# Two score blocks in one tick: head pairs of a projection group in a hybrid attention layer

## The chip, the cores and the metric

One core of a Trainium2 chip runs the whole program. The metric is the device time of one execution in microseconds (us), as the median of three runs. Beside the timed runs there is one execution under the hardware profiler; its rows give the start and length of every instruction of each engine.

## The reference

A decoder layer on 256 tokens of width 2048, in float32. Two groups of 16 heads of 64 stand side by side: group A attends in a sliding window of 128 with two shared key and value heads, ALiBi slopes and a learned sink per head; group B attends causally over all 256 tokens with a forget gate per head. Then come an output projection and a channel mixer.

```python
q_a, k_a, v_a, q_b, k_b, v_b, f_b = jnp.split(rmsnorm(x, g) @ w_in, cuts, axis=-1)
# group A, per head:  s = q k^T / 8 - slope * distance, inside the window
p = exp(s - m) / (sum(exp(s - m)) + exp(sink - m));  o_a = p v
# group B, per head:  s = q k^T / 8 + c[t] - c[s],  c = cumsum(log_sigmoid(f_b + b))
p = softmax(s);  o_b = p v
mix = concat(rmsnorm(o_a), rmsnorm(o_b)) @ w_out
x = x + rmsnorm(mix)
x = x + rmsnorm((gelu(conv(gate)) * conv(val)) @ w_down)
```

## The kernel before, in words

All large products are float32 products made of parts. A weight unit of 128 x 1024 floats is loaded from memory by the SP queue into one of five `raw` buffers; ScalarE (ACT) casts it to a high part `whi` (L112) and VectorE (DVE) subtracts to get a low part `wlo` (L115), each with five buffers. TensorE (PE) multiplies high by the high and low halves of the activations in one product of 512 columns (L253) and low by high in one of 256 columns (L258).

`proj_T` computes 256 output columns: in each of its two halves stand 16 products of L253 and 16 of L258, and four calls of `tick()`: after 6 and 12 of the L253, after 10 of the L258, and at the half's end, so eight ticks in all. The value projections (L309, `mm3`) and the output projection have ticks of their own. A tick runs whatever was registered for it by `later(n, f)`. In this way attention work is put in the middle of a projection, and since the PE queue is in program order, the tick fixes where it stands there. DVE, ACT, GpSimd (POOL) and SP get their order from a scheduler that moves with the program; each then executes in that order and waits in place.

A projection group makes the queries of 256 columns, which are two head pairs; there are four groups in each attention group. `attend` registers four steps for a pair at the ticks that `stages` gives:

- `tables`, three ticks ahead of the scores: POOL writes the bias of the pair into `p` (two buffers). In group B this begins with a small load `cb` (L578) on the SP queue, also two buffers.
- `scores` (L475): twelve small products on 64 rows, six for each head `e`, into two of the four PSUM banks tagged `att`. Then DVE adds the bias and takes the row maximum (L481, four of them), ACT takes the exponentials (L493, four), DVE adds the sink in group A (L489, L496), inverts the sums (L497) and scales `p` (L500, four).
- `transposes` (L510): six on PE into two `att` banks; ACT casts the high part `ph` (L312), DVE makes the low part `pl` (L313).
- `pv` (L522 and L524 in group A, L534 and L536 in group B): the value products into one `att` bank; ACT and DVE move the result to `oT` (L527, L530, L545, L546, L547), and POOL sums the squares (L551, L553).

Before the change `stages(n)` puts scores, transposes and value products at ticks n, n + 6 and n + 9. In group A the pairs have n = 6, 14, 22 and so on, eight ticks apart; in group B the first pair of a group has n = 3 and the second 11, counted from the end of the group's key projection, the second falling in the next projection. Queries and keys are moved out of PSUM by L440 (ACT), L441 (DVE) and L442 (POOL), and split by L312 and L313; a key pair takes one of three slots of the tile `keys`.

Of the kernel before, what the change touches and what calls it, by code (L numbers as in the profile page):

```python
# [31 lines left out]
def hybrid_layer(ctx: ExitStack, tc: tile.TileContext, x, pre_mix_g, w_in, b_forget, sinks,  # L32
# [16 lines left out]
    def bank(tag="acc"):  # L49
        return ps.tile([P, 512], F32, tag=tag, bufs=4, name="bank_" + tag)  # L50
# [9 lines left out]
    def later(n, f):  # L60
        todo.setdefault(now[0] + n, []).append(f)
# [116 lines left out]
    def rstd_of(ssq, n, out_tag):  # L178

        v = small.tile([P, 1], F32, tag="rv", name="rv")  # L180
        dve.tensor_scalar(v, ssq, 1.0 / n, EPS, op0=ALU.mult, op1=ALU.add)
        r = small.tile([P, 1], F32, tag=out_tag, bufs=2, name=out_tag)
        pool.tensor_tensor(r, v, mhalf, op=ALU.pow)
        return r
# [58 lines left out]
    def proj_T(w, c0, banks):  # L243

        for v in (0, 2):
            parts = [w_split(w_load(w_rows(w, u * 4, 4, c0, 256), 4, 256), still=True)
                     for u in (v, v + 1)]
            steps = [(u, a) for u in range(2) for a in range(4)]

            def high(u, a):  # L250
                kt = (v + u) * 4 + a
                for m, b in enumerate(banks):
                    pe.matmul(b, parts[u][0][:, a, m * P:(m + 1) * P], hT[:, kt, :],  # L253
                              start=(kt == 0), stop=(kt == KT - 1))

            def low(u, a):
                for m, b in enumerate(banks):
                    pe.matmul(b[:, 256:512], parts[u][1][:, a, m * P:(m + 1) * P],  # L258
                              hT[:, (v + u) * 4 + a, 0:256], start=False, stop=False)

            for n, (u, a) in enumerate(steps[:-1]):
                high(u, a)
                if n in (2, 5):
                    tick()
            for n, (u, a) in enumerate(steps):
                low(u, a)
                if n == 4:
                    tick()
            high(*steps[-1])
            tick()  # L270
# [40 lines left out]
    def split(hi, lo, src):  # L311
        act.copy(hi, src)  # L312
        dve.tensor_tensor(lo, src, hi.bitcast(F32), op=ALU.subtract)  # L313

    with tc.tile_pool(name="mixp", bufs=1) as mp:
# [37 lines left out]
        def scratch():  # L353
            rot[0] += 1
            i = 6 + rot[0] % 10
            return scr[:, i * 256:(i + 1) * 256]
# [80 lines left out]
        def evac_sum(b, dst, row):  # L437

            c = scratch()
            act.copy(c, b[:, 256:512])  # L440
            dve.tensor_tensor(dst, b[:, 0:256], c, op=ALU.add)  # L441
            pool.tensor_tensor(dst, dst, row, op=ALU.mult)  # L442

        def q_pair(b):
            q = scratch()
            evac_sum(b, q, rowq)
            qh = ap.tile([P, 256], F32R, tag="qh", bufs=6, name="qh")
            ql = ap.tile([P, 256], F32R, tag="ql", bufs=6, name="ql")
            split(qh, ql, q)
            return qh, ql  # L450

        def k_pair(b, i):
            k = scratch()
            evac_sum(b, k, rowk)
            split(khi[i], klo[i], k)
# [106 lines left out]
        def swa_pair(p, q, at):  # L562
            def table(t):
                for e in range(2):
                    slope = 2.0 ** (-8.0 * (2 * p + e + 1) / H)
                    pool.tensor_scalar(t[:, e, 0:256], dist, -slope, None, op0=ALU.mult)
                    pool.tensor_scalar(t[:, e, 256:384], dist[:, P:256], -slope, None,
                                       op0=ALU.mult)

            attend(p, q, p // 4, lambda t: vpa[:, t, p // 4, :], table, 2 * p, True, at,  # L570
                   True)
# [3 lines left out]
        def fox_pair(p, q, ki, at):  # L575
            def table(t):
                cb = ap.tile([P, 2, 256], F32, tag="cb", bufs=2, name="cb")
                sp.dma_start(cb.rearrange("p e k -> p (e k)"),  # L578
                             c_dram[2 * p:2 * p + 2, :].rearrange("e k -> (e k)")
                             .partition_broadcast(P))  # L580
                for e in range(2):
                    h = 2 * p + e
                    pool.tensor_scalar(t[:, e, 0:256], cb[:, e, :], -1.0, cq[:, 1, h:h + 1],
                                       op0=ALU.mult, op1=ALU.add)
                    pool.tensor_scalar(t[:, e, 256:384], cb[:, e, 0:P], -1.0, cq[:, 0, h:h + 1],
                                       op0=ALU.mult, op1=ALU.add)

                v = t[:, :, P:384]
                pool.affine_select(out=v, in_=v, compare_op=ALU.is_ge, fill=NEG, base=0,
                                   pattern=[[0, 4], [-1, P]], channel_multiplier=1)  # L590

            attend(8 + p, q, ki, lambda hl, t: vpb[:, hl, t, p, :], table, 2 * p, False, at)

        def stages(n):
            return n, n + 6, n + 9


        def kv_a():
# [21 lines left out]
        for g in range(4):  # L620
            if g == 0:
                b2 = bq0
            else:
                b2 = [bank(), bank()]
                proj_T(w_in, g * 256, b2)
            for m in range(2):
                swa_pair(2 * g + m, q_pair(b2[m]), stages(6 + 8 * (2 * g + m) - 8 * g))


        z = ap.tile([P, 2, H], F32, tag="z", name="z")  # L630
        for p0, npair, cols in ((0, 3, 384), (3, 3, 384), (6, 2, 272)):
            b2 = [bank(), bank()]
# [45 lines left out]
        def group_rstd(i, into):  # L678
            gbk = bank("att")
            for t in range(2):  # L680
                pe.matmul(gbk[:, t:t + 1], sqs[:, i, t * P:(t + 1) * P], ones[:, 0:1],
                          start=True, stop=True)
            for t in range(2):
                into.append(rstd_of(gbk[:, t:t + 1], 1024, f"rg{i}{t}"))

        rstd_a, rstd_b = [], []
        later(30, lambda: group_rstd(0, rstd_a))
        for g in range(4):
            bq = [bank(), bank()]
            proj_T(w_in, 1280 + g * 256, bq)  # L690
            qs = [q_pair(b) for b in bq]
            bk = [bank(), bank()]
            proj_T(w_in, 2304 + g * 256, bk)
            for m in range(2):
                ki = (2 * g + m + 2) % NK
                k_pair(bk[m], ki)
                fox_pair(2 * g + m, qs[m], ki, stages(3 + 8 * m))


        later(stages(11)[2] + 4, lambda: group_rstd(1, rstd_b))  # L700
        mix_sb = main.tile([P, 2, D], F32, tag="y", name="mix_sb")
        mix = [[mix_sb[:, t, n * 512:(n + 1) * 512] for n in range(4)] for t in range(2)]

# [528 lines left out]
```

## Time and profile before

| what | value |
|---|---|
| median of 3 runs | 1070.96 us (1070.4 to 1071.1) |
| the profiled execution | 1070.95 us |
| its span, first to last instruction | 1069.2 us |
| PE busy over the span | 1052.4 us, 98% |
| DVE busy | 843.4 us, 79% |
| ACT busy | 637.2 us, 60% |
| POOL busy | 224.8 us, 21% |
| mean granted TensorE clock | 0.997 |

The profiled execution agrees with the median to 0.01 us; 1.75 us of it lie outside the span. Attention work stands between 42 and 275 us: group A from 42 to 149 us, group B from 161 to 274 us. In a row of the timeline the first number is the start, the second the length of the merged row, then engine, line and tiles, and a count; a square bracket gives the idle time before it and what ended it. PE records overlap, because a product starts before the one ahead of it has ended, so the pace of PE is read from starts to starts and not from lengths.

### The profile page before, as it was taken

To read this page: it belongs to the slowest core of one execution; us is meant where nothing else is said; L and a number is where in the kernel's file an instruction comes from. 1 tells how busy PE (TensorE), PEld (TensorE's weight loads), DVE (VectorE), ACT (ScalarE), POOL (GpSimd) and SP (SyncE) were. 2 spreads that over 40 slices of the span, in tenths; PEclk is the share of its full clock that TensorE was granted. 3 is DMA by queue.
4 is the path that set the end of the run, shared out by engine and by line. 5 is a ranking of instruction groups with operands and counts; after the bars stand their busy time and mean duration, and the time that the engine had idled before them with its cause. 6 is when DMAs were issued, how large, how long until landed. Compare 5 with 4: busy or idle time off the path is not lost.

```text
span 1069.2 us, 16290 instructions
## 1 busy us (share of the span) xinstructions
PE 1052.4 (98%) x5890; PEld 912.9 (85%) x5890; DVE 843.4 (79%) x1369; ACT 637.2 (60%) x1096; POOL 224.8 (21%) x256
## 2 busy tenths in 40 slices
PE   9999999999999999999999999999999999999996
PEld 7889988887889988888888888888888888888785
DVE  5988877887567887787767989668777787788995
ACT  7766766666556765565655556446555565656561
POOL 3233343342022121221212000002121211200202
PEclk9999999999999999999999999999999999999998
DMA  8645657555873776665666566666566666685552
GB/s 291 206 120 174 180 160 210 161 153 156 300 248 106 266 229 188 192 190 181 211 186 191 192 203 209 215 187 197 167 209 190 190 191 195 192 301 191 167 175 79
DMA packets 154284, 207.08 MB, mean 194 GB/s; under 512 B 6844, under 2 KB 131036, under 8 KB 153180
## 3 DMA queue, kind: packets, MB, share of 16 engines
q1 hardware_dynamic: 153200, 203.37, 60.5%
q10 hardware_dynamic: 1004, 2.68, 0.6%
q8 instruction: 46, 0.75, 0.3%
q14 instruction: 34, 0.28, 0.1%
HBM read 201.68 MB, written 4.21 MB: 193 GB/s over the span
## 4 chain that ended last, share of the span: by engine, by line
PE 90%; DVE 4%; DMA 2%; issue 2%; POOL 1%; ACT 1%; SPq 0%; DVEq 0%; POOLq 0%; ACTq 0%
PE bank_acc L284 16%; PE bank_att L967 14%; PE bank_att L284 14%; PE bank_acc L309 12%; PE bank_acc L290 8%; PE bank_att L290 7%; PE bank_acc L253 6%; PE bank_acc L967 4%; PE bank_acc L258 3%; PE bank_att L475 1%; DVE wlo L313 1%; PE bank_att L510 1%; DVE wlo L115 1%; PE bank_acc L932 1%; DMA x_in<-in_x_dram 1%
## 5 line engine op out<-in xcount | busy, mean ns | idle before, releaser
L115 DVE TENSOR_TENSOR wlo<-raw,whi 128x1024 fp32r<-128x1024 f32 (+3 forms) x271 | 330.1, 1228 | 117.1 <-ACT whi L112 112.4
L112 ACT CAST whi<-raw 128x1024 fp32r<-128x1024 f32 (+3 forms) x270 | 273.3, 1029 | 124.4 <-issue 88.9
L899 POOL TENSOR_TENSOR room<-room,rowf 128x256 f32<-128x256 f32 x88 | 100.3, 1160 | 393.9 <-DVE room L898 392.1
L284 PE MATMUL bank_acc<-hT,whi 128*128 128x512 f32 x736 | 173.3, 390 | 0.0
L284 PEld LDWEIGHTS bank_acc<-hT,whi 128*128 128x128 f32 x736 | 136.5, 188 | 27.3
L967 PE MATMUL bank_att<-whi,G 128*128 128x512 f32 x488 | 156.2, 389 | 0.0
L284 PE MATMUL bank_att<-hT,whi 128*128 128x512 f32 x640 | 150.6, 390 | 0.0
L284 PEld LDWEIGHTS bank_att<-hT,whi 128*128 128x128 f32 x640 | 118.7, 188 | 23.8
L967 PEld LDWEIGHTS bank_att<-whi,G 128*128 128x128 f32 x488 | 91.6, 188 | 18.9
L967 PE MATMUL bank_att<-wlo,G 128*128 128x512 f32 x244 | 95.2, 390 | 2.4 <-DVE wlo L313 2.4
L290 PEld LDWEIGHTS bank_acc<-hT,wlo 128*128 128x128 f32 x736 | 89.3, 188 | 2.0
L290 PE MATMUL bank_acc<-hT,wlo 128*128 128x256 f32 x736 | 89.9, 279 | 0.0
L253 PE MATMUL bank_acc<-hT,whi 128*128 128x512 f32 x352 | 89.2, 396 | 0.0
L901 ACT ACTIVATE room<-room,cw 128x256 f32<-128x256 f32 x88 | 53.0, 602 | 60.6 <-POOL room L899 60.6
L309 PE MATMUL bank_acc<-whi,oT 128*128 128x512 f32 (+1 forms) x272 | 82.5, 380 | 0.0
L290 PEld LDWEIGHTS bank_att<-hT,wlo 128*128 128x128 f32 x640 | 77.6, 188 | 1.7
L290 PE MATMUL bank_att<-hT,wlo 128*128 128x256 f32 x640 | 77.9, 279 | 0.0
L903 DVE SCALAR_TENSOR_TENSOR room<-room,cw 128x256 f32<-128x256 f32 x88 | 62.4, 709 | 17.5 <-ACT room L901 17.3
L313 DVE TENSOR_TENSOR wlo<-raw,whi 128x1024 fp32r<-128x1024 f32 (+1 forms) x56 | 62.4, 1138 | 13.4 <-ACT whi L312 13.4
L253 PEld LDWEIGHTS bank_acc<-hT,whi 128*128 128x128 f32 x352 | 63.0, 188 | 11.3
L312 ACT CAST whi<-tb 128x1024 fp32r<-128x1024 f32 x42 | 44.0, 1050 | 45.0 <-PE bank_att L967 19.2
L312 ACT CAST whi<-raw 128x1024 fp32r<-128x1024 f32 (+1 forms) x56 | 52.4, 958 | 28.8 <-PE bank_att L967 22.2
(254 smaller groups left out, 1589.9 us busy)
## 6 DMA issues: line engine op xcount, KB each, us to landing
raw<-in_w_up_dram SPq DMA_DIRECT2D x176, 512.0 KB, 4.1
raw<-in_w_down_dram SPq DMA_DIRECT2D x58, 512.0 KB, 4.8
raw<-in_w_in_dram SPq DMA_DIRECT2D x51, 512.0 KB, 3.9
raw<-in_w_out_dram SPq DMA_DIRECT2D x32, 512.0 KB, 4.7
extra<-in_w_down_dram SPq DMA_DIRECT2D x20, 512.0 KB, 3.8
raw<-in_w_in_dram SPq DMA_DIRECT2D x16, 384.0 KB, 3.4
tb<-in_w_down_dram SPq DMA_DIRECT2D x10, 512.0 KB, 4.8
cb<-c_dram SPq DMA_DIRECT2D x8, 256.0 KB, 3.6
```

Of the source, the lines that this page charges most:

```text
L112: i1 = act.copy(hi[:, cs], raw[:, cs])
L115: i2 = dve.tensor_tensor(lo[:, cs], raw[:, cs], hi[:, cs].bitcast(F32), op=ALU.subtract)
L253: pe.matmul(b, parts[u][0][:, a, m * P:(m + 1) * P], hT[:, kt, :], start=(kt == 0), stop=(kt == KT - 1))
L284: pe.matmul(b, parts[u][0][:, a, m * P:(m + 1) * P], hT[:, kt, :], start=(kt == 0), stop=(kt == KT - 1))
L290: pe.matmul(b[:, 256:512], parts[u][1][:, a, m * P:(m + 1) * P], hT[:, kt, 0:256], start=False, stop=False)
L309: pe.matmul(b, a, r[:, cols], start=(first and i == 0), stop=(last and i == 2))
L312: act.copy(hi, src)
L313: dve.tensor_tensor(lo, src, hi.bitcast(F32), op=ALU.subtract)
L899: pool.tensor_tensor(u[:, 2:258], u[:, 2:258], rowf, op=ALU.mult)
L901: act.activation(y, u[:, 2:258], AF.Identity, bias=cw[:, 3, ch:ch + 1], scale=cw[:, 2, ch:ch + 1])
L903: dve.scalar_tensor_tensor(y, u[:, 1:257], cw[:, 1, ch:ch + 1], y, op0=ALU.mult, op1=ALU.add)
L967: pe.matmul(b[:, to] if to else b, a, r[:, cols], start=(first and i == 0), stop=(last and i == 2))
```

## The change

`stages` takes the pair's place m in its group. Both pairs of a group get the same n; the second pair has its transposes and value products four ticks behind those of the first. In group A n is 6 for the first group, 14, 22 and 30 for the next, counted from each group's projection; in group B it is 6.

```diff
-        def stages(n):
-            return n, n + 6, n + 9
+        def stages(n, m):
+            return n, n + 6 + 4 * m, n + 9 + 4 * m
...
-                swa_pair(2 * g + m, q_pair(b2[m]), stages(6 + 8 * (2 * g + m) - 8 * g))
+                swa_pair(2 * g + m, q_pair(b2[m]), stages(6 + 8 * g, m))
...
-                fox_pair(2 * g + m, qs[m], ki, stages(3 + 8 * m))
+                fox_pair(2 * g + m, qs[m], ki, stages(6, m))
...
-        later(stages(11)[2] + 4, lambda: group_rstd(1, rstd_b))
+        later(stages(6, 1)[2] + 4, lambda: group_rstd(1, rstd_b))
```

In ticks from the end of a group's projection, group A of the first group goes from scores 6 and 14, transposes 12 and 20, values 15 and 23 to scores 6 and 6, transposes 12 and 16, values 15 and 19. Group B goes from scores 3 and 11, transposes 9 and 17, values 12 and 20 to 6 and 6, 12 and 16, 15 and 19. No instruction is added or removed; the last sum of squares on PE (L681) comes one tick earlier.

On PE, in the first group of group A, the last scores of the first pair (`qh_464`) were followed by the projection:

```order
L475 MATMUL bank_att_559<-keys_440,ql_465 128x128
L475 MATMUL bank_att_558<-keys_440,qh_464 128x128
L475 MATMUL bank_att_559<-keys_440,qh_464 128x128
L253 MATMUL bank_acc_475<-hT_111,whi_539 128x512
L253 MATMUL bank_acc_476<-hT_111,whi_539 128x512
```

Now those of the second pair (`qh_471`) follow at once, in two more banks:

```order
L475 MATMUL bank_att_564<-keys_440,ql_465 128x128
L475 MATMUL bank_att_563<-keys_440,qh_464 128x128
L475 MATMUL bank_att_564<-keys_440,qh_464 128x128
L475 MATMUL bank_att_596<-keys_440,qh_471 128x256
L475 MATMUL bank_att_597<-keys_440,qh_471 128x256
```

Twelve score products have moved up to stand behind the first twelve; the same is done in all eight groups.

On DVE, in the same group, this stood between the first pair's row maxima and the low part of its transposes (`pl`):

```order
L115 TENSOR_TENSOR wlo<-raw,whi 128x1024
L489 TENSOR_TENSOR es<-nm,snk 128x4
L441 TENSOR_TENSOR scr<-bank_acc,scr 128x256
L496 TENSOR_TENSOR rs<-rs,es 128x4
L441 TENSOR_TENSOR scr<-bank_acc,scr 128x256
L497 RECIPROCAL rs<-rs 128x4
L500 TENSOR_SCALAR p<-p,rs 128x256 x2
L500 TENSOR_SCALAR p<-p,rs 128x128 x2
L313 TENSOR_TENSOR ql<-scr,qh 128x256 x2
L115 TENSOR_TENSOR wlo<-raw,whi 128x1024 x3
L313 TENSOR_TENSOR pl<-bank_att,ph 128x384 x2
```

Now the first pair's softmax and the second pair's row maxima come first, and this stands between them and the same `pl`, with L489, L496, L497 and L500 of the second pair:

```order
L115 TENSOR_TENSOR wlo<-raw,whi 128x1024
L489 TENSOR_TENSOR es<-nm,snk 128x4
L441 TENSOR_TENSOR scr<-bank_acc,scr 128x256 x2
L115 TENSOR_TENSOR wlo<-raw,whi 128x1024
L496 TENSOR_TENSOR rs<-rs,es 128x4
L313 TENSOR_TENSOR ql<-scr,qh 128x256
L497 RECIPROCAL rs<-rs 128x4
L313 TENSOR_TENSOR ql<-scr,qh 128x256
L500 TENSOR_SCALAR p<-p,rs 128x256 x2
L500 TENSOR_SCALAR p<-p,rs 128x128 x2
L115 TENSOR_TENSOR wlo<-raw,whi 128x1024 x2
L313 TENSOR_TENSOR pl<-bank_att,ph 128x384 x2
```

The four L115 between the first row maximum and `pl` are as many as before; the second pair's whole softmax has come ahead of the first pair's `pl`.

On DVE in group B, the second pair's result (`oT9`) was moved out by L547 behind the softmax of the next group's first pair (`p_2340`):

```order
L481 ISA p_2340,nm_2382<-bank_att_2369,p_2340 128x128
L481 ISA nm_2382 128x1
L497 RECIPROCAL rs_2387<-rs_2387 128x4
L500 TENSOR_SCALAR p_2340<-p_2340,rs_2387 128x256 x2
L500 TENSOR_SCALAR p_2340<-p_2340,rs_2387 128x128 x2
L115 TENSOR_TENSOR wlo_2595<-raw_2592,whi_2594 128x1024
L547 SCALAR_TENSOR_TENSOR oT9_124<-bank_att_2406,gcol_107,oT9_124 64x256 x2
```

Now it stands ahead of that softmax (`p_2373`):

```order
L115 TENSOR_TENSOR wlo_2522<-raw_2519,whi_2521 128x1024
L115 TENSOR_TENSOR wlo_2528<-raw_2525,whi_2527 128x1024
L547 SCALAR_TENSOR_TENSOR oT9_124<-bank_att_2359,gcol_107,oT9_124 64x256
L115 TENSOR_TENSOR wlo_2580<-raw_2577,whi_2579 128x1024
L547 SCALAR_TENSOR_TENSOR oT9_124<-bank_att_2359,gcol_107,oT9_124 64x256
L481 ISA p_2373,nm_2439<-bank_att_2425,p_2373 128x256
```

The evacuation of the value bank and the next row maxima have changed places.

## The prediction

> **What bounds the kernel now.** I read the page first, then PE's waits, then the timeline of PE and DVE around single attention steps.
>
> ```profile
> PE 1052.4 (98%) x5890; PEld 912.9 (85%) x5890; DVE 843.4 (79%) x1369; ACT 637.2 (60%) x1096; POOL 224.8 (21%) x256
> ```
>
> PE is busy through 98% of the span. A time can only fall where PE stands still or runs slower than its pace. The list of PE's waits has two entries in the attention steps:
>
> ```profile
> PE bank_att L475 <- ACT keys L312: 1.2, 1, 1.2
> ...
> PE bank_att L475 <- DVE keys L313: 0.8, 1, 0.8
> ```
>
> Both are scores of group B that wait for keys. The rest has to be read from the distance of starts. A stretch of plain projection, then the transposes of a pair (L510) and projection again:
>
> ```profile
> 58.84 3.81 PE L253 MATMUL bank_acc<-hT,whi 128*128 128x512 f32 x16
> 62.48 2.03 PE L258 MATMUL bank_acc<-hT,wlo 128*128 128x256 f32 x16
> 64.35 0.63 PE L253 MATMUL bank_acc<-hT,whi 128*128 128x512 f32 x2
> 64.81 0.82 PE L510 MATMUL bank_att<-ident,p 128*128 128x128 f32 x6
> 65.39 0.95 PE L253 MATMUL bank_acc<-hT,whi 128*128 128x512 f32 x3
> ```
>
> Sixteen L253 take 62.48 - 58.84 = 3.64 us, 0.2275 each; sixteen L258 take 64.35 - 62.48 = 1.87, 0.117 each. Half a projection is 5.51 us. Six transposes take 0.58. Now the second pair's scores in the first group of group A, up to the first pair's value product (L522):
>
> ```profile
> 53.62 1.29 PE L253 MATMUL bank_acc<-hT,whi 128*128 128x512 f32 x5
> 54.84 0.39 PE L475 MATMUL bank_att<-keys,qh 64*128 64x256 f32 x2
> ...
> 55.48 0.28 PE L475 MATMUL bank_att<-keys,qh 64*128 64x128 f32 x2
> 55.68 0.74 PE L253 MATMUL bank_acc<-hT,whi 128*128 128x512 f32 x2
> 56.26 1.33 PE L258 MATMUL bank_acc<-hT,wlo 128*128 128x256 f32 x10
> 57.43 0.39 PE L522 MATMUL bank_att<-ph,vpa 128*128 128x512 f32 x1
> ```
>
> From 53.62 to 56.26 are 2.64 us, of which seven L253 at pace are 1.59. The block of twelve scores costs 1.05 us. Inside it, 54.84 to 55.48 is 0.64 up to the last pair of products, so at its own rate the block is about 0.75; the other 0.30 lies at its two ends, where products on 64 rows meet products on 128.
>
> **What the change takes away.** In each of the eight groups two such blocks become one, with two ends instead of four. The second block then costs 0.75 instead of 1.05: 8 x 0.30 = 2.4 us off PE. Bounds: 0.2 to 0.32 a group, the lower if the step from one pair's operands to the other's costs 0.1 of its own, so 1.6 to 2.6.
>
> The waits for keys in group B, in the first group and in the last:
>
> ```profile
> 158.87 1.33 PE L258 MATMUL bank_acc<-hT,wlo 128*128 128x256 f32 x10
> 161.44 0.39 PE L475 MATMUL bank_att<-keys,qh 64*128 64x256 f32 x2 [1.24 <-ACT keys L312]
> ...
> 162.57 0.62 PE L258 MATMUL bank_acc<-hT,wlo 128*128 128x256 f32 x3
> ```
>
> ```profile
> 243.78 0.39 PE L475 MATMUL bank_att<-keys,qh 64*128 64x256 f32 x2
> ...
> 245.66 0.51 PE L309 MATMUL bank_acc<-whi,oT 128*128 128x512 f32 x1
> ```
>
> Ten L258 from 158.87 end at 160.04 by their pace. A block's start costs 0.08 more (54.84 against 53.62 + 5 x 0.2275 above), so the scores could stand at 160.12; they stand at 161.44, 1.32 late. The block lasts 162.57 - 161.44 = 1.13 where an undisturbed one lasts 55.68 - 54.84 = 0.84, 0.29 more. The other lasts 1.88, 1.04 more. Together 2.65 us. The scores move from tick 3 to tick 6. In a projection that is the rest of the first half (six L258 and two L253, 1.16) and twelve L253 of the second (2.73), 3.9 us, against 1.6 of lateness; in the output projection three ticks of six 512-column products are 4.1 against 1.0. I take all 2.65 as gone. Next late there are the second pair's keys, which are evacuated right behind the first pair's and have the same new margin, less what they come later.
>
> **What it adds.** Three things have to be ready sooner, relative to the work in front of them: the low part `pl` of the first pair's transposes, the fourth `att` bank, and the tables of the second pair.
>
> *`pl` in the first group of group A.* DVE before:
>
> ```profile
> 44.68 0.47 DVE L481 CUSTOM_DVE_ANT_0 p<-bank_att,p,nsnk 128x256 f32<-128x256 f32 x1
> ...
> 46.03 1.21 DVE L115 TENSOR_TENSOR wlo<-raw,whi 128x1024 fp32r<-128x1024 f32 x1
> ...
> 53.88 1.01 DVE L313 TENSOR_TENSOR pl<-bank_att,ph 128x384 fp32r<-128x384 f32 x2
> ```
>
> `pl` is done at 54.89, with no idle time in this stretch. The changed order puts the second pair's softmax in front of it: four L481 (46.03 - 44.68 = 1.35), L489, L496 and L497 (0.18 each by the L497 row below, 0.54), four L500 (1.01, below), and the wait for the first pair's exponentials, which an L115 hid: 1.17 by the row below, of which L489 and one L481 still cover 0.56, so 0.6. Sum 3.5, `pl` at 58.4. On PE the same work as before precedes the value product, less 0.30, so it starts at 57.13, and its second product, which reads `pl`, at 57.36. PE waits about 1.0; some small waits for ACT and POOL between queries and splits are not in this sum, so I take 1.2, between 0.4 and 1.8. In the later groups of group A DVE starts in time, and I count nothing.
>
> *`pl` in group B.* Here DVE is the engine to watch:
>
> ```profile
> 188.78:216.41 27.63, 27.63 (x178) 24.20 (x178) 22.54 (x48) 17.57 (x43) 10.36 (x15) 1.00 0.55 165
> ```
>
> The third pair of numbers after the duration is DVE: 22.54 of 27.63 us in one group, at a granted clock of 1.00. What it does for one pair (and, from group A, how soon a row maximum starts behind its scores, 55.79 - 54.84 = 0.95):
>
> ```profile
> 190.89 0.41 DVE L481 CUSTOM_DVE_ANT_0 p<-bank_att,p 128x256 f32<-128x256 f32 x1
> ...
> 193.24 0.18 DVE L497 RECIPROCAL rs<-rs 128x4 f32<-128x4 f32 x1 [1.17 <-ACT p L493]
> 193.45 1.01 DVE L500 TENSOR_SCALAR p<-p,rs 128x256 f32<-128x256 f32 x4
> ...
> 196.79 0.49 DVE L547 SCALAR_TENSOR_TENSOR oT<-bank_att,gcol,oT 64x256 fp32r<-64x256 f32 x1 [0.81 <-ACT sqo L546]
> ...
> 198.69 0.76 DVE L441 TENSOR_TENSOR scr<-bank_acc,scr 128x256 f32<-128x256 f32 x2
> 199.36 1.64 DVE L115 TENSOR_TENSOR wlo<-raw,whi 128x1024 fp32r<-128x1024 f32 x1
> 200.93 0.95 DVE L313 TENSOR_TENSOR ql<-scr,qh 128x256 fp32r<-128x256 f32 x1
> ...
> 202.45 1.02 DVE L313 TENSOR_TENSOR pl<-bank_att,ph 128x384 fp32r<-128x384 f32 x2
> ```
>
> ```profile
> 55.79 0.48 DVE L481 CUSTOM_DVE_ANT_0 p<-bank_att,p,nsnk 128x256 f32<-128x256 f32 x1 [0.90 <-PE bank_att L475]
> ```
>
> From the first row maximum to the first pair's `pl` the new order has eight L481 (twice 193.24 - 1.17 - 190.89 = 1.18), the wait of 1.17 less one L481, 0.8, two L497 (0.4), eight L500 (2.0), two L441 (0.76), two query splits (202.45 - 200.93 = 1.5), four L115 (1.4 each, between 1.21 and 1.64: 5.6) and `pl` (1.0): 14.5 us, and 0.95 in front, 15.4 us after the scores begin. PE reaches the product that needs it after the merged scores (1.6, with 0.1 behind), four L253 and sixteen L258 (2.78), half a projection (5.51), transposes (0.67), fourteen L253 and ten L258 (4.36) and two value products (0.46): 15.5 us. It just fits. With all L115 at 1.64 it is late by 0.9, with all at 1.21 early by 0.8. I take 0.3 for each of the three groups inside projections, 0.9 in all, bounds 0 and 2.7. What speaks for less: the new order fills DVE's waits of 1.17 and 0.81 per pair with other work.
>
> *Cheap ones.* The second pair's bias takes POOL time earlier, and its `cb` load goes to the SP queue one or two weight loads sooner, where it waits for a buffer of the pair before. Weight loads queue behind it. They run far ahead, and the list of waits charges L115 with 0.2 us on PE, so nothing is counted; without that cover a load would cost PE its own few microseconds.
>
> **The sum.** 1070.95 (the profiled execution; the median of the runs is 1070.96) - 2.4 - 2.65 + 1.2 + 0.9 = 1068.0 us.
>
> **Rivals.**
>
> *No new waits.* If DVE keeps ahead at both places, 1070.95 - 5.05 = 1065.9. For it speaks that DVE's waits are filled; against it, that nothing in the first group gives DVE time. Chance 0.15.
>
> *The fourth bank.* The second pair's scores need four banks at once; the fourth was last used by the value product of the previous group's second pair. From that product's start to the need are 1.05 (itself), 1.16, 2.73 and 0.75 us, 5.7 in all.
>
> ```profile
> 190.89 0.62 PE L534 MATMUL bank_att<-ph,vpb 128*128 128x512 f32 x2
> ...
> 191.94 2.43 PE L253 MATMUL bank_acc<-hT,whi 128*128 128x512 f32 x10
> ```
>
> Evacuation took 197.28 - 190.89 = 6.4. If it stays so, each of three groups waits 0.7, and the time is 1068.0 + 2.1 = 1070.1, no change. Against it: L547 now stands ahead of the next row maxima. Chance 0.18.
>
> *Slower: VectorE and GpSimd in each other's way.* The place is the same chain to `pl` in group B.
>
> ```profile
> 199.19 2.41 POOL L442 TENSOR_TENSOR scr<-scr 128x256 f32<-128x256 f32 x2 [1.61 <-DVE scr L441]
> 201.59 0.64 POOL L583 TENSOR_SCALAR p<-cb,cq 128x256 f32<-128x256 f32 x1
> ...
> 203.62 0.64 POOL L589 TENSOR_SCALAR_AFFINE_SELECT p<-p 128x512 f32<-128x512 f32 x1
> ```
>
> Beside the two L442 an L115 took 1.64 instead of 1.21. POOL's work in the chain is 2.41 and a table of 203.62 + 0.64 - 201.59 = 2.67, 5.1 us. If DVE had to wait all of it out, the chain would be 14.5 - 0.8 (already in the four L115) + 5.1 = 18.8, and with the 0.95 in front PE would be late by 4.25 in each of three groups, 12.8 us: 1070.95 - 5.05 + 1.2 + 12.8 = 1079.9. It makes the kernel slower from a chain of 16.5 us on, where the three waits reach 2.0 each. Against it: the measured loss beside POOL is 0.43 on an L115 of that length. Chance 0.1. The Trainium skill (SBUF — State Buffer, Who interferes with whom) has the rule behind it: VectorE instructions with two inputs in SBUF and GpSimd instructions that read SBUF take turns on a shared port, and the later one is blocked completely; the rows show less than that, 0.43 us beside a GpSimd pair of 2.41.
>
> *The change does not do what it says on PE.* If the 0.30 belongs to each pair's twelve scores and not to the ends of a block, 2.4 us of the gain are missing: 1068.0 + 2.4 = 1070.4. Against it stands where the time lies, 0.08 ahead of the block and 0.12 in the two L253 behind it (56.26 - 55.68 against 2 x 0.2275). The Trainium skill (TensorEngine Tiling (Array Packing), Key Properties) says that a change of tiling mode drains TensorE. By that rule the ends are what costs, and the trace agrees with its 0.08 and 0.12. Chance 0.05.
>
> **How the numbers follow.** The forecast has 0.52. A measurement of this kernel tells 0.2%, 2.1 us, from no change. Faster than 1068.8: the forecast for the most part (0.47) and no new waits (0.15), 0.62. Within: the rest of the forecast, the fourth bank and the change that does nothing, 0.28. Slower: 0.1. The range goes from 1065.8 (no new waits) to 1071.5 (both waits at their upper bounds, 1.8 and 2.7, and 2.1 for the bank: 1070.95 - 5.05 + 6.6 = 1072.5, not all at once); it leaves out the slower case and some of the fourth bank.
>
> **What would show it.** Right: 24 score products in about 1.6 us, no entry for `keys` among PE's waits, one wait of about 1.2 us at L522 for `pl` near 57 us, and short ones at L534. Wrong: a wait at L475 for L547 or L546 (fourth bank), waits over 2 us at L534 (slower), or projection products beside merged scores that lose as much as two blocks did.

## The result, and the profile after

| | median | range | runs |
|---|---|---|---|
| before | 1071.28 us | 1070.33 to 1073.34 | 12 |
| after | 1068.78 us | 1067.68 to 1070.0 | 12 |

The ratio is 0.9974 with a 95% interval of 0.9966 to 0.9982, so 2.8 us less, between 1.9 and 3.6. The forecast was 1068.0 us, 2.95 us less. The profiled execution after took 1069.6 us, with a span of 1067.9.

The busy shares have hardly moved (PE 1051.7 us and 98% as before, DVE 839.9 and 79%); the change is 2.8 us in one stage. To see that stage by itself, two fixed points on PE are taken: the first product of the first projection (L253) and the first product of the channel mixer (L932). Between them lies all attention work; outside them the program is unchanged. Ahead of the colon in these groups of instructions are line, operation and count; the two numbers of "first and last start" stand behind the three durations. Before:

```profile
L932 PE MATMUL bank_acc<-hT,whi x64: 274/283/364, 336.9 to 350.7; 128*128 128x256 f32 x64
L253 PE MATMUL bank_acc<-hT,whi x352: 386/390/504, 32.6 to 238.7; 128*128 128x512 f32 x176
```

After:

```profile
L932 PE MATMUL bank_acc<-hT,whi x64: 274/283/364, 334.5 to 348.3; 128*128 128x256 f32 x64
L253 PE MATMUL bank_acc<-hT,whi x352: 387/389/525, 33.0 to 237.7; 128*128 128x512 f32 x176
```

The stage took 336.9 - 32.6 = 304.3 us before and 334.5 - 33.0 = 301.5 after: 2.8 less. This stage time is read to 0.1 us, and a second profile of the kernel before gives 304.1; it is the measure of all that follows. That the spans differ by 1.3 only has two reasons outside the stage: the start was 0.4 us later, and late in the down projection the granted clock of TensorE fell. In these windows of the changed kernel the clock is the number behind the five busy times:

```profile
1002.00:1004.00 2.00, 1.66 (x6) 0.85 (x5) 2.00 (x3) 0.04 (x1) 0.19 (x1) 0.58 0.71 252
1004.00:1006.00 2.00, 2.00 (x7) 1.56 (x6) 2.00 (x3) 1.01 (x1) 0.00 (x0) 0.56 0.71 193
```

The scores of two pairs in group B, in the timeline of PE after:

```profile
191.30 2.20 PE L253 MATMUL bank_acc<-hT,whi 128*128 128x512 f32 x9
193.43 0.38 PE L475 MATMUL bank_att<-keys,qh 64*128 64x256 f32 x2
...
194.97 0.73 PE L253 MATMUL bank_acc<-hT,whi 128*128 128x512 f32 x2
195.53 1.22 PE L258 MATMUL bank_acc<-hT,wlo 128*128 128x256 f32 x9
```

The 24 products last 194.97 - 193.43 = 1.54 us. Ahead of them nine L253 took 2.13 instead of 9 x 0.2275 = 2.05, and the two L253 behind took 0.56 instead of 0.455. With both ends the block costs 1.72, against twice 1.05 before: about 0.38 less in each group by these rows.

PE's waits in the attention steps, after (engine and tile, then total, times, longest in us):

```profile
PE bank_att L522 <- DVE pl L313: 1.3, 2, 0.7
...
PE bank_att L475 <- DVE gcol L410: 0.5, 1, 0.5
```

The two entries for keys are gone. There are waits for `pl` at two places, and one that the forecast did not have. The first is in group A's first group:

```profile
42.46 0.39 PE L475 MATMUL bank_att<-keys,qh 64*128 64x256 f32 x2
...
44.05 0.38 PE L475 MATMUL bank_att<-keys,qh 64*128 64x256 f32 x1 [0.52 <-DVE gcol L410]
...
44.88 0.53 PE L253 MATMUL bank_acc<-hT,whi 128*128 128x512 f32 x1
...
58.37 0.40 PE L522 MATMUL bank_att<-ph,vpa 128*128 128x512 f32 x1
59.34 0.50 PE L522 MATMUL bank_att<-pl,vpa 128*128 128x512 f32 x1 [0.58 <-DVE pl L313]
...
59.91 0.86 PE L258 MATMUL bank_acc<-hT,wlo 128*128 128x256 f32 x6
```

The bracket gives idle time between records, and records overlap, so what a wait costs is read from starts. The block of scores lasts 44.88 - 42.46 = 2.42 us instead of 1.53: 0.9 lost. The second pair's scores are the first to need all four `att` banks at once, and one of them still held the gains' transposes, which DVE copies to `gcol` (L410). The value product lasts 59.91 - 58.37 = 1.54 instead of the 0.70 of a free one: 0.85 lost. DVE in front of it:

```profile
43.82 0.18 DVE L410 COPY gcol<-bank_att 128x32 f32<-128x32 f32 x1
43.92 1.21 DVE L115 TENSOR_TENSOR wlo<-raw,whi 128x1024 fp32r<-128x1024 f32 x1
45.06 0.47 DVE L481 CUSTOM_DVE_ANT_0 p<-bank_att,p,nsnk 128x256 f32<-128x256 f32 x1
...
58.28 1.01 DVE L313 TENSOR_TENSOR pl<-bank_att,ph 128x384 fp32r<-128x384 f32 x2
```

From the first row maximum to the end of `pl` are 59.29 - 45.06 = 14.2 us. The other place is the value product of the second pair in the last group of A:

```profile
141.59 0.40 PE L522 MATMUL bank_att<-ph,vpa 128*128 128x512 f32 x1
142.72 0.50 PE L522 MATMUL bank_att<-pl,vpa 128*128 128x512 f32 x1 [0.73 <-DVE pl L313]
...
143.38 0.61 PE L665 MATMUL bank_att<-scr,lf 128*16 128x256 f32 x2
```

It lasts 1.79 us to the gate's first product; without a wait it would be 0.78 (0.70, and 0.08 more because the last product's step to L665 takes 0.20 instead of 0.12): 1.0 lost.

Group B has no wait. DVE and PE there, after:

```profile
194.38 0.42 DVE L481 CUSTOM_DVE_ANT_0 p<-bank_att,p 128x256 f32<-128x256 f32 x1 [0.72 <-PE bank_att L475]
...
206.41 1.01 DVE L313 TENSOR_TENSOR pl<-bank_att,ph 128x384 fp32r<-128x384 f32 x2
```

```profile
208.42 0.62 PE L534 MATMUL bank_att<-ph,vpb 128*128 128x512 f32 x2
208.88 0.39 PE L534 MATMUL bank_att<-pl,vpb 128*128 128x512 f32 x1
```

`pl` is done at 207.42, 13.0 us after the first row maximum, and is needed at 208.88: 1.5 us to spare.

### The profile page after: what moved, and what is told of

It reads as the page before. It is cut to its first block, busy times and chain, and to the rows that moved or that the text cites. A ratio compares the mean times of both kernels' runs of the same rounds, so it can differ in the third digit from the quotient of the medians.

```text
span 1067.9 us, 16269 instructions
## 1 busy us (share of the span) xinstructions
PE 1051.7 (98%) x5890; PEld 914.4 (86%) x5890; DVE 839.9 (79%) x1369; ACT 640.1 (60%) x1096; POOL 230.1 (22%) x256
## 3 DMA queue, kind: packets, MB, share of 16 engines
q10 hardware_dynamic: 1004, 2.68, 0.6%
## 4 chain that ended last, share of the span: by engine, by line
PE 86%; DVE 8%; issue 2%; DMA 1%; ACT 1%; POOL 1%; SPq 0%; DVEq 0%; POOLq 0%; ACTq 0%
PE bank_acc L284 15%; PE bank_att L284 14%; PE bank_acc L309 13%; PE bank_att L967 11%; PE bank_acc L290 8%; PE bank_att L290 7%; PE bank_acc L253 7%; PE bank_acc L258 3%; PE bank_acc L967 3%; DVE wlo L313 2%; PE bank_att L475 1%; PE bank_att L510 1%; DVE wlo L115 1%; PE bank_acc L932 1%; DMA extra<-in_w_down_dram 1%
## 5 line engine op out<-in xcount | busy, mean ns | idle before, releaser
L115 DVE TENSOR_TENSOR wlo<-raw,whi 128x1024 fp32r<-128x1024 f32 (+3 forms) x271 | 327.7, 1221 | 124.3 <-ACT whi L112 116.1
L253 PE MATMUL bank_acc<-hT,whi 128*128 128x512 f32 x352 | 88.6, 396 | 0.0
L313 DVE TENSOR_TENSOR wlo<-raw,whi 128x1024 fp32r<-128x1024 f32 (+1 forms) x56 | 62.4, 1138 | 14.5 <-ACT whi L312 14.5
L253 PEld LDWEIGHTS bank_acc<-hT,whi 128*128 128x128 f32 x352 | 63.2, 188 | 11.7
```

The costliest lines, as they stand in the source:

```text
L115: i2 = dve.tensor_tensor(lo[:, cs], raw[:, cs], hi[:, cs].bitcast(F32), op=ALU.subtract)
```

## The experiments

The theory after the result: merging takes two ends of a block off PE in each group, the later place in group B takes the waits for keys away, and the price is paid in group A's first and last group, where DVE is late for three steps. The rivals to it: the 0.30 belongs to the pairs and not to the ends; DVE is late as a whole there, so that a wait removed turns up at the next step; the parts do not add up, since each group shifts the next.

All are measured against the kernel before: the ratio of the timed runs with its 95% interval, and the stage time from one profile each (starts of L253 and L932, as above; before 304.3 us).

| kernel | ratio (95%) | L253, L932 start | stage, against before |
|---|---|---|---|
| after | 0.9974 (0.9966 to 0.9982) | 33.0, 334.5 | -2.8 |
| group B alone merged | 0.9954 (0.9943 to 0.9966) | 32.6, 332.8 | -4.1 |
| group B late, not merged | 0.9971 (0.9962 to 0.9981) | 32.6, 334.2 | -2.7 |
| second scores a tick later | 1.0009 (0.9999 to 1.0018) | 32.8, 338.6 | +1.5 |
| `gcol` copied by ScalarE | 0.9962 (0.9950 to 0.9974) | 32.8, 334.0 | -3.1 |
| two value products a tick later | 0.9950 (0.9934 to 0.9966) | 33.7, 333.4 | -4.6 |
| both of these | 0.9949 (0.9932 to 0.9966) | 32.4, 331.4 | -5.3 |
| group B and A's inner groups | 0.9944 (0.9928 to 0.9961) | 32.6, 332.0 | -4.9 |
| group A alone merged | 0.9986 (0.9974 to 0.9997) | 32.6, 335.4 | -1.5 |
| first keys by VectorE | 0.9987 (0.9977 to 0.9997) | 32.6, 335.6 | -1.3 |
| before once more | one run | 32.6, 336.7 | -0.2 |

The timed runs agree with the stage times within their intervals, which reach 0.9 to 1.8 us to either side; differences among the experiments are read from the stage, with one profile for each kernel and a second one for before. Differences near 0.2 us, by which the two profiles of before differ, say nothing by themselves. A start that is late by itself does not shorten the stage: with two value products a tick later it is at 33.7, and the first scores stand 9.5 us behind it, as before.

**Group B alone merged.** Against the changed kernel:

```diff
-                swa_pair(2 * g + m, q_pair(b2[m]), stages(6 + 8 * g, m))
+                swa_pair(2 * g + m, q_pair(b2[m]), stages(6 + 16 * g + 8 * m - 8 * g, 0))
```

> The two pairs of a group are merged in group B alone; group A is as in the kernel before. Theory (merging is worth 0.33 us a group by the ends of the blocks, the key waits of 2.65 us lie in group B, and all three new waits, 0.90 + 0.62 + 0.78 us, lie in group A): 4 x 0.33 + 2.65 = 4.0 us less than before, about 1.2 us less than the changed kernel, and none of the waits for gcol or pl in group A among PE's waits. Rival (the new waits in group A only show a lateness that VectorE has anyway, and it turns up elsewhere): the same as or slower than the changed kernel, 1.5 to 2.8 us less than before.

The stage took 4.1 us less than before, 1.3 less than the changed kernel; no wait for `gcol` or `pl` is left. The theory held: beside the merged group B, merging group A costs 1.3 us.

**Group B late, not merged.** Against the changed kernel; the ticks come out as in the kernel before, but with group B three ticks later:

```diff
-                swa_pair(2 * g + m, q_pair(b2[m]), stages(6 + 8 * g, m))
+                swa_pair(2 * g + m, q_pair(b2[m]), stages(6 + 16 * g + 8 * m - 8 * g, 0))
...
-                fox_pair(2 * g + m, qs[m], ki, stages(6, m))
+                fox_pair(2 * g + m, qs[m], ki, stages(6 + 8 * m, 0))
...
-        later(stages(6, 1)[2] + 4, lambda: group_rstd(1, rstd_b))
+        later(stages(14, 0)[2] + 4, lambda: group_rstd(1, rstd_b))
```

> The kernel before, with the pairs of group B three ticks later (scores at ticks 6 and 14 instead of 3 and 11), nothing merged. Theory (the waits for keys go by the later place alone and cost nothing else): 2.65 us less than before; the blocks of twelve scores keep their cost of 1.03 to 1.05 us; no entry for keys among PE's waits. Rival (the waits for keys gave VectorE time, and without them PE waits for pl or a bank instead): 0 to 1 us less than before. Second rival (the waits go only because the blocks are merged): 0.

2.7 us less: the two waits for keys were worth what the trace of before showed, and no other wait took their place. Group B alone merged differs from this kernel by the merging, and by the second pair's transposes and value products, which come four ticks earlier with it; PE waits for neither of these in either kernel. 4.1 - 2.7 = 1.4 us for four groups, 0.35 each: that is the price of two ends, and the starts above give nearly the same.

**Second scores a tick later.** Against the changed kernel:

```diff
-            return n, n + 6 + 4 * m, n + 9 + 4 * m
+            return n + m, n + 6 + 4 * m, n + 9 + 4 * m
```

> The changed kernel, with the scores of the second pair one tick behind those of the first, so that each group has two blocks of twelve again; all else is as in the changed kernel. Theory (a block's two ends cost 0.33 us): 8 x 0.33 = 2.7 us more than the changed kernel, less the wait for the bank of gcol in the first group of group A (0.90 us), which a tick takes away: 1.8 us more than the changed kernel, 1.0 less than before. Rival (the 0.30 us belong to each pair's twelve scores, not to the ends): two blocks cost what one of 24 did, and with the bank wait gone it is 0.9 us less than the changed kernel.

4.3 us more than the changed kernel, not 1.8. PE in group A's first group:

```profile
44.87 0.39 PE L475 MATMUL bank_att<-keys,qh 64*128 64x256 f32 x2
...
45.71 0.50 PE L258 MATMUL bank_acc<-hT,wlo 128*128 128x256 f32 x2
...
57.71 0.50 PE L522 MATMUL bank_att<-ph,vpa 128*128 128x512 f32 x1
59.76 0.50 PE L522 MATMUL bank_att<-pl,vpa 128*128 128x512 f32 x1 [1.54 <-DVE pl L313]
...
60.33 0.87 PE L258 MATMUL bank_acc<-hT,wlo 128*128 128x256 f32 x6
```

The second block is again one of twelve that lasts 0.84, and the ends are back: 8 x 0.35 = 2.8; the wait for the bank is gone, -0.9. What the theory missed are the waits for `pl`. The second pair's softmax now starts a tick later (its first row maximum at 49.05 instead of 46.60) and still stands ahead of the first pair's `pl` on DVE. Between the first row maximum and this `pl` DVE stands idle for ScalarE for 2.2 us, against 0.65 in the changed kernel; the longest of these waits:

```profile
55.98 0.43 DVE L313 TENSOR_TENSOR ql<-scr,qh 128x256 fp32r<-128x256 f32 x1 [1.06 <-ACT qh L312]
```

The value product lasts 60.33 - 57.71 = 2.62, 1.1 more than in the changed kernel, the one in the last group of A lasts 2.50 (143.48 to 145.98), 0.7 more, and a new one in the second group lasts 1.17 instead of 0.71, 0.5 more. The sum is 2.8 - 0.9 + 2.3 = 4.2. The rival (0.30 belongs to each pair) falls. So scores in one tick give two things: two ends fewer and, by these rows, an earlier start of the second softmax, with which DVE waits less for ScalarE.

**`gcol` copied by ScalarE.** Against the changed kernel:

```diff
-            dve.tensor_copy(gcol[:, 16:48], gb2[:, :32])
+            act.copy(gcol[:, 16:48], gb2[:, :32])
```

> The changed kernel, with the copy of gcol out of its bank on ScalarE instead of VectorE. Theory A (VectorE's queue is what paces the first group of group A; the wait for the bank only hides part of the lateness of pl): the wait of 0.90 us at the second pair's scores goes, the wait for pl at L522 grows from 0.62 to 1.3 to 1.5 us, and the time falls by 0 to 0.2 us against the changed kernel. Theory B (the two waits are independent): the wait for pl stays at 0.6 and the time falls by 0.9 us.

0.3 us less than the changed kernel. The 24 scores of the first group now last 1.53, from 42.26 to 43.79, and the value product waits longer:

```profile
57.26 0.40 PE L522 MATMUL bank_att<-ph,vpa 128*128 128x512 f32 x1
58.82 0.50 PE L522 MATMUL bank_att<-pl,vpa 128*128 128x512 f32 x1 [1.17 <-DVE pl L313]
...
59.39 0.87 PE L258 MATMUL bank_acc<-hT,wlo 128*128 128x256 f32 x6
```

59.39 - 57.26 = 2.13, so 1.43 lost here instead of 0.9 + 0.85. The two lengths together give the same 0.3 less as the stage. That is near theory A: the two waits were for the most part one lateness of DVE, and PE paid it in two places.

**Two value products a tick later.** Against the changed kernel:

```diff
-        def stages(n, m):
-            return n, n + 6 + 4 * m, n + 9 + 4 * m
+        def stages(n, m, late=0):
+            return n, n + 6 + 4 * m, n + 9 + 4 * m + late
...
-                swa_pair(2 * g + m, q_pair(b2[m]), stages(6 + 8 * g, m))
+                swa_pair(2 * g + m, q_pair(b2[m]), stages(6 + 8 * g, m, int((g, m) in ((0, 0), (3, 1)))))
```

> The changed kernel, with the value products of two pairs a tick later: the first pair of group A's first group and the second pair of its last. Theory (the two waits for pl, 0.85 and about 1.0 us by the length of their blocks, are a due time that lies too early, and nothing behind it is late): both waits go, since a tick is 1.16 us of projection in the first place and the gate's products and 0.46 us more in the second; 1.8 us less than the changed kernel; the wait of 0.90 for the bank of gcol stays. Rival (VectorE is late as a whole there, and what waits moves on to the next product that reads from it: the second pair's transposes or pl, the gate's lf): 0 to 0.5 us less than the changed kernel, with a new entry among PE's waits.

1.8 us less than the changed kernel, as the theory said. The value product in the first group:

```profile
60.24 0.40 PE L522 MATMUL bank_att<-ph,vpa 128*128 128x512 f32 x1
60.47 0.39 PE L522 MATMUL bank_att<-pl,vpa 128*128 128x512 f32 x1
```

The products follow at 0.23, the pace of PE, and in the last group too; nothing behind them waits instead. The block of the first 24 scores still lasts 2.42, so the wait for the copy of `gcol` stays. Apart from it, DVE was late for these two steps and for nothing else.

**Both.** The two edits above together.

> The changed kernel with gcol copied by ScalarE and the two value products a tick later. Theory (with the copy on ScalarE the wait for pl in the first group is 1.43 us; a tick of 1.16 us covers all of it but about 0.3; the wait in the last group goes): 0.90 + 0.85 + 1.0 - 0.3 = 2.4 us less than the changed kernel, about 5.2 us less than the kernel before, and the fastest of all. Rival (VectorE is late as a whole): no more than 0.5 us less than the changed kernel with the copy on ScalarE, about 3.5 us less than before.

5.3 us less than before, 2.5 less than the changed kernel: the theory held. What is left of the first group's wait:

```profile
57.96 0.40 PE L522 MATMUL bank_att<-ph,vpa 128*128 128x512 f32 x1
58.39 0.50 PE L522 MATMUL bank_att<-pl,vpa 128*128 128x512 f32 x1
...
58.96 0.82 PE L510 MATMUL bank_att<-ident,p 128*128 128x128 f32 x6
```

1.00 instead of 0.70: the 0.3 expected. By the stage this kernel is faster than with either edit alone; by the timed runs it cannot be told from the one before it, nor from the next one.

**Group B and A's inner groups.** Against the changed kernel:

```diff
-                swa_pair(2 * g + m, q_pair(b2[m]), stages(6 + 8 * g, m))
+                swa_pair(2 * g + m, q_pair(b2[m]), stages(6 + 8 * g, m) if g in (1, 2) else stages(6 + 8 * g + 8 * m, 0))
```

> Merged in group B and in the second and third group of group A; the first and the last group of A as in the kernel before. Theory (a merged group is worth 0.355 us, by the kernel merged in B alone against the kernel with B late; no new wait arises in A's inner groups): 6 x 0.355 + 2.65 = 4.8 us less than before, 0.7 less than with group B alone merged. Rival (merging in A costs VectorE its lead everywhere, and a wait for pl appears in the second, third or last group): equal to or slower than group B alone, 4.1 us less than before or worse.

4.9 us less than before, 0.8 less than group B alone. Merging is worth its 0.35 us in the inner groups of A as well; only its first and its last group lost by it.

**Group A alone merged.** Against the changed kernel, group B as before:

```diff
-                fox_pair(2 * g + m, qs[m], ki, stages(6, m))
+                fox_pair(2 * g + m, qs[m], ki, stages(3 + 8 * m, 0))
...
-        later(stages(6, 1)[2] + 4, lambda: group_rstd(1, rstd_b))
+        later(stages(11, 0)[2] + 4, lambda: group_rstd(1, rstd_b))
```

> Merged in group A alone; group B is as in the kernel before, waits for keys included. Theory (the parts add up: four merged groups take 4 x 0.355 = 1.4 us away, the waits for the bank of gcol and twice for pl add 0.90 + 0.85 + 1.0 = 2.7): 1.3 us more than the kernel before, 0.12% slower. Rival (what PE loses in group A gives group B's keys the time that they lack, so that the waits for keys shrink by as much): no more than 0.3 us from the kernel before.

1.5 us less than before, where the theory had 1.3 more. All three waits in group A are there, but both waits for keys are gone, though group B is untouched: 1.3 - 2.65 = -1.35. The rival's mechanism is there, and it was given too small a size, but something else came with it. The first keys' row factor is multiplied in by POOL (L442), behind the first bias tables, and these wait for the load `cb`. POOL before:

```profile
152.65 0.77 POOL L583 TENSOR_SCALAR p<-cb,cq 128x256 f32<-128x256 f32 x1 [4.95 <-DMA cb<-c_dram]
...
160.23 1.40 POOL L442 TENSOR_TENSOR scr<-scr 128x256 f32<-128x256 f32 x2
```

With group A alone merged:

```profile
150.37 1.45 POOL L583 TENSOR_SCALAR p<-cb,cq 128x256 f32<-128x256 f32 x1 [2.22 <-DMA cb<-c_dram]
...
157.94 2.42 POOL L442 TENSOR_TENSOR scr<-scr 128x256 f32<-128x256 f32 x2
```

The SP queue issued `cb` at 147.05 instead of 148.97, and the tables began 2.3 earlier, while PE came 1.2 later (its scores could stand at 160.12 before and start at 161.37 now). The store of `c` that `cb` reads landed after 2.0 us instead of 4.3; why is open. So GpSimd came to the keys 2.3 earlier (157.94 instead of 160.23) and PE 1.2 later, and either would have taken nearly all of the first wait of 1.32; this run does not tell them apart. The last wait is taken up in the section on the hardware.

**First keys by VectorE.** Against the kernel before, in `evac_sum` and `k_pair`, for the first group of B alone:

```diff
-            pool.tensor_tensor(dst, dst, row, op=ALU.mult)
+            (eng or pool).tensor_tensor(dst, dst, row, op=ALU.mult)
...
-                k_pair(bk[m], ki)
+                k_pair(bk[m], ki, dve if g == 0 else None)
```

> The kernel before, with the row factor of the first two pairs' keys of group B multiplied in on VectorE instead of GpSimd (two instructions of 128x256); nothing else differs. Theory (the first wait for keys comes from GpSimd's queue, where the first tables stand ahead of the keys' product and wait for the cb load; the last one is VectorE's lateness that this first wait leaves and that grows by 0.55 us a pair): both waits go, 2.6 us less than before, and the row maxima of group B start no more than 1.6 us behind their scores instead of 2.0 to 4.6. Rival 1 (two causes): the first wait alone goes, 1.6 us less, and the last one of about 1.0 stays. Rival 2 (PE has no time to gain there, the scores wait for VectorE in any case): no change.

1.3 us less: the first wait goes, so POOL's queue was its cause, and the last one stays and is a little longer (its block lasts 2.11 instead of 1.88). PE, then DVE behind the first and the last of these scores:

```profile
160.05 0.39 PE L475 MATMUL bank_att<-keys,qh 64*128 64x256 f32 x2
...
243.80 0.45 PE L475 MATMUL bank_att<-keys,qh 64*128 64x256 f32 x4 [0.94 <-DVE keys L313]
```

```profile
161.13 0.42 DVE L481 CUSTOM_DVE_ANT_0 p<-bank_att,p 128x256 f32<-128x256 f32 x1
...
247.12 0.41 DVE L481 CUSTOM_DVE_ANT_0 p<-bank_att,p 128x256 f32<-128x256 f32 x1
```

The first row maximum stands 161.13 - 160.05 = 1.1 us behind its scores, the last 247.12 - 242.29 = 4.8 (the last block starts at 242.29). Rival 1 was right: these are two causes. DVE's lateness in group B grows from pair to pair even when it starts on time.

**Before once more.** No edit.

> The kernel before once more, for a second profile. Theory (the two waits for keys belong to the program, not to one execution): the same two waits at L475, 1.2 and 0.8 us by the list, the same block of 1.88 us in the last group. Rival (they are an accident of that execution, of the landing of a load): other waits, or none.

```profile
PE bank_att L475 <- ACT keys L312: 1.1, 1, 1.1
...
PE bank_att L475 <- DVE keys L313: 0.8, 1, 0.8
```

Both waits are there again, and the last block lasts 1.91. They belong to the program.

## Why the prediction was right, step by step

| step | forecast | measured | by |
|---|---|---|---|
| ends of blocks | -2.4 (-1.6 to -2.6) | -2.8 | 8 x 0.35, B merged against B late |
| waits for keys | -2.65 | -2.7 | B late |
| first group of A | +1.2 (0.4 to 1.8) | +1.75 | 0.9 at the bank, 0.85 at `pl` |
| last group of A | 0 | +1.0 | its block; with the 0.85, 1.8 in the value products moved |
| `pl` in group B | +0.9 (0 to 2.7) | 0 | the profile after |
| sum | -2.95 | -2.75 | stage: -2.8 |

- **Ends of blocks.** The mechanism was right and the term a little small: 0.35 a group, above the bound of 0.32. The step from one pair's operands to the other's, for which the lower bound set 0.1 aside, costs about 0.04 (1.54 for 24 products against twice 0.75). Why an end costs what it does was not tried by a run.
- **Waits for keys.** All 2.65 went, and the second pair's keys were not late next. But the margin is not the only remedy: group A alone merged and the first keys on VectorE show that the first wait hangs on when GpSimd gets to the keys, and the last on how late DVE has become in group B.
- **First group of A.** The forecast had DVE's chain from the first row maximum to `pl` at 58.4 - 44.7 = 13.7 us; it took 14.2. The "other end" of the same lateness was not seen: the bank that the copy of `gcol` held. The fourth bank was a rival, but in group B, with the value product of the previous group in it. It decided in the first group of A, where the bank's last user stood behind a queue of DVE work. With the copy on ScalarE the wait at `pl` alone is 1.43, inside the bounds, so the sum of the step was sound and its place half wrong.
- **Last group of A.** Here a step failed: "In the later groups of group A DVE starts in time, and I count nothing." That is so in the second and third group. In the last, the second pair's value product had come four ticks earlier, and DVE has the values of group B and the gate in front of `pl`. It stands idle there for one of them:

```profile
137.51 0.19 DVE L661 SCALAR_TENSOR_TENSOR lf<-z,az 128x32 f32<-128x32 f32 x1 [0.97 <-ACT az L659]
```

- **`pl` in group B.** Forecast 14.5 us of chain, measured 13.0. Each query split took 0.33 from start to start instead of the 0.75 that rows of before gave, where POOL was at work beside the first and 0.19 us of idle time for ScalarE was counted in; L115 took 1.13, 1.69 and twice 1.13 from start to start, 5.1 in all instead of 5.6; the rest is overlap of short instructions. The bound with every L115 at 1.21 would have said that no wait comes.
- **Rivals.** The slower one did not come: DVE's chain of 13.0 us stayed far from 16.5. "No new waits" failed by 2.75 us. That the change does nothing on PE is refuted by group B alone merged and by the second scores a tick later.

So the mechanism of the gain was right, and the total was right to 0.2 us by luck: two of its terms were wrong by about the same amount in opposite directions, 0.9 in group B that did not come and 1.0 in the last group of A that was not looked for, and so were two smaller ones, 0.4 more at the ends and 0.55 more in the first group of A. Merged everywhere, with two due times and one copy moved, the same idea gives 5.3 us.

## What to carry to other kernels

When a step is moved so that it needs more buffers at once, go through the last user of every buffer at the first place where the new number is reached, not only in the steady state; the first and the last group of a loop have other neighbours, and here they alone paid. Where one engine's lateness is paid for by another at two waits, taking one of them away moves it to the other; give the late step a later due time instead. And a stage measured between two unchanged instructions resolves a few tenths of a microsecond, which the whole time does not.

## What the runs showed of the hardware that was not expected

**Turns of VectorE and GpSimd.** The prediction read from an L115 of 1.64 us beside GpSimd's L442 that one loses only 0.43 to the other. The rows show full turns, and GpSimd pays more. Before, at the last keys:

```profile
242.48 1.66 DVE L115 TENSOR_TENSOR wlo<-raw,whi 128x1024 fp32r<-128x1024 f32 x1
```

```profile
242.31 2.41 POOL L442 TENSOR_TENSOR scr<-scr 128x256 f32<-128x256 f32 x2 [1.62 <-DVE scr L441]
```

With group A alone merged:

```profile
240.29 1.66 DVE L115 TENSOR_TENSOR wlo<-raw,whi 128x1024 fp32r<-128x1024 f32 x1 [0.60 <-ACT whi L112]
```

```profile
239.44 1.43 POOL L442 TENSOR_TENSOR scr<-scr 128x256 f32<-128x256 f32 x2 [1.69 <-DVE scr L441]
240.87 1.69 POOL L583 TENSOR_SCALAR p<-cb,cq 128x256 f32<-128x256 f32 x1
```

There L115 waits 0.6 us for ScalarE, both L442 come in ahead and take 1.43, and it is L583 that stands until L115 ends at 241.95 and takes 0.61 more, 1.69 instead of the 0.64 it takes alone. Before, L115 stands between the two L442, which take 2.41: it ends at 244.14, and the second L442 0.58 later, at 244.72. The Trainium skill (SBUF — State Buffer, Who interferes with whom) says that the port pair which VectorE shares with GpSimd is an exclusive lock, that a VectorE instruction with two inputs in SBUF contends there with a GpSimd instruction that reads SBUF, and that the order of issue decides who blocks. The rows agree with it, more than the prediction allowed. So the keys come 1.0 us later in each turn of before. There DVE's lateness grows, from 2.0 us behind the scores in the second pair of group B to 4.6 in the seventh; with group A alone merged it does not, and the row maximum of the last group's first scores stands 244.87 - 243.43 = 1.4 us behind them. The turn on the port does not explain this by itself: from its first L441 to `pl` DVE takes 3.76 us in a turn of before (198.69 to 202.45) and 3.81 with group A alone merged (197.48 to 201.29). It loses the time between `pl` and the next row maximum, 2.81 us (202.45 to 205.26) against 2.12 (201.29 to 203.41): the L115 there waits 0.30 for ScalarE and takes 1.56 instead of 1.26. Whether the later keys bring that about was not tried by a run.

**The clock.** The granted clock of TensorE fell to 0.58 and 0.56 for four microseconds near 1004 us in the changed kernel's profile, and cost the run about 1.1 us there (PE was 2.4 us ahead of before at 1003 us and 1.2 at 1006). Before, it was 1.00 in the same stretch, with as much idle time on PE just ahead of it (2.4 us in two waits, against 2.3). The same fall stands in the profile of the first keys by VectorE, where nothing is merged (0.59 from 1004 to 1008 us), and in neither of the two profiles of before; its cause is open. So the spans of single executions can differ by that much without any merging.
